# A hybrid trunk layer on one core: the first block normalised in two halves of 256 tokens, and the steps' chain moved beside the first pair of weight tiles

## The chip, the core and the metric

The kernel runs on one core of a Trainium2 chip. The metric is the device time of one execution in microseconds (us). Engines are named PE (TensorE), DVE (VectorE), ACT (ScalarE), POOL (GpSimd) and SP (SyncE, which issues all the DMAs here). PEld is PE's loading of weights, which overlaps its products.

## The reference

One layer on 2048 tokens of width 1024, all in float32:

```
h    = rmsnorm(x, norm_mix_w)
u_b, u_c, u_h, z, xbc, dt_raw = split(h @ w_in)
y_a  = u_b * conv3(u_c * u_h)                        # short gated convolution
xbc  = silu(conv4(xbc) + b);  dt = softplus(dt_raw + dt_bias)
y_b  = rmsnorm((ssd_scan(xs, dt, -exp(a_log), B, C) + d_skip * xs) * silu(z))
x    = x + concat(y_a, y_b) @ w_out
x    = x + relu(rmsnorm(x, norm_mlp_w) @ w_up)**2 @ w_down
out  = rmsnorm(x, final_norm_w)
```

where `rmsnorm(x, w) = x / sqrt(mean(x*x) + 1e-5) * w`.

## The kernel before

Channels lie on the 128 partitions, tokens along a tile. Tokens are worked in blocks of 512 (TB), two blocks to a half (TH = 1024). A float32 operand is split into a high part, rounded to a reduced form that PE takes in one pass (float32r), and the rest as a low part; one product is then three matmuls: high by high, low by high, high by low (`mm3`). Weight tiles are loaded whole (`load_w`), ACT casts the high part (`split_w`, line 103) and DVE subtracts to get the low part (line 104). Activations are split the same way (`split`, lines 204 and 205).

Most of the input projection works on *pairs* of weight tiles with seven products instead of eight per 2x2 block (`chain`), in the order of the list `PAIRS`: 'ch' pairs make the short convolution's input, 'x' pairs the four-tap convolution's (`conv`), 'b' and 'z' pairs the gates. For each pair the next pair's weights are combined and split (`weights`, `combine`). Beside the first pairs `prepare` normalises the second half's blocks, one step after each of the seven products of a pair (`late` in `first_half`); in the last pair of the list the blocks of the next half are fetched and split (`refresh`).

Before the first pair stands `start`: it loads x block 0, three weight tiles (z columns 24 to 26), squares block 0 on ACT, adds the squares on DVE, and sums over partitions on PE with `ones` as the moving column (`Rstd.reduce`). `Rstd.root` takes the root on ACT and the reciprocal on DVE, splits it into two float32r parts and spreads each over a diagonal; `Rstd.spread` turns the diagonals into a row that is alike in all partitions, with two matmuls, and copies it to SBUF. The block is multiplied by that row and split, eight tiles one after another. Then PE multiplies three weight tiles at once for block 0 (`group`), a fourth with its own accumulator, and the same for block 1; `begin_block(1)` normalises block 1 beside it and `begin_sums` builds the sums of blocks that the seven products want. `dt_part` is the chain of the steps (dt): 16 narrow products on PE, transposes, a softplus of some 25 small DVE operations, decays, and stores; block 0's chain runs inside `start`, block 1's mostly beside the first pair.

At the end `norm_out` uses the same `root` and `spread` for the final norm of the last block and of its two last halves of 256 tokens.

The order on each engine is made by a scheduler from the order in which the program writes the instructions, and from what it takes each to last. The pool `utmp` has four buffers, `e` five, `wraw` three; PSUM's eight banks are named mm (three), mw, yo, yd (one each) and tp (two).

Of the kernel before, what the change touches and what calls it, by code (L numbers as in the profile page):

```python
# [16 lines left out]
P = 128  # L17
T = 2048
# [21 lines left out]
def trunk(ctx: ExitStack, tc: tile.TileContext, x, w_in, w_dt, w_out, w_up, w_down, cvec, hrow, out):  # L40
# [31 lines left out]
    nc.sync.dma_start(cv[:, 0:NCV], cvec)  # L72
# [12 lines left out]
    nc.scalar.copy(cv[:, NCV + 1 : NCV + 2], eps)  # L85
# [21 lines left out]
    def take(it, n=None):  # L107

        return list(itertools.islice((w for w in it if w is not None), n))

# [10 lines left out]
    class Rstd:  # L121
# [18 lines left out]
        def root(self):  # L140
            n = self.n
            r = self.pool.tile([P, n], F32, tag="rs", name="rs", bufs=2)
            nc.scalar.activation(r, self.sums, AF.Sqrt, bias=eps, scale=self.scale)
# [4 lines left out]
            self.diag = []  # L148
            for i in range(2):
                diag = self.tmp("diag")[:, 0 : self.w].bitcast(F32R)  # L150
                nc.vector.tensor_tensor(
                    out=diag.rearrange("p (c t) -> p c t", c=n),
                    in0=ident.unsqueeze(1).to_broadcast([P, n, P]),
                    in1=r2[:, i, :].bitcast(F32).unsqueeze(2).to_broadcast([P, n, P]),
                    op=ALU.mult,
                )
                self.diag.append(diag)
# [16 lines left out]
        def spread(self, rb=None):  # L174
            prb = self.ps = psum("tp", "prb", 2)[:, 0 : self.w]
            for i in range(2):
                nc.tensor.matmul(prb, ones_r, self.diag[i], start=(i == 0), stop=(i == 1))
# [12 lines left out]
    class Seven:  # L190
# [10 lines left out]
        def split(self, pair, i, t):  # L201

            hi, lo = (x[:, i] for x in pair)
            nc.scalar.copy(hi, t)  # L204
            nc.vector.tensor_tensor(out=lo, in0=t, in1=hi.bitcast(F32), op=ALU.subtract)
# [92 lines left out]
        def fill(self, n, k, t):  # L298
# [5 lines left out]
            self.split(p[i], j, t)  # L304
# [99 lines left out]
    class Proj(Seven):  # L404
# [4 lines left out]
        PAIRS = "ch0 ch1 b0 x0 x8 ch2 ch3 b2 x2 ch4 ch5 b4 x4 x10 ch6 ch7 b6 x6 z4 z6".split()  # L409
# [41 lines left out]
        def begin_block(self, bb):  # L451
# [4 lines left out]
            for m, t in enumerate(xt):  # L456
                if bb == 0:
                    sq = self.wide("sq")
                    nc.scalar.activation(sq, t, AF.Square)
                    sq = [sq[:, 0], sq[:, 1]]  # L460
                else:
                    sq = [acc if m + i == 0 else self.tmp("sq") for i in range(2)]
                    for i in range(2):
                        nc.scalar.activation(sq[i], t[:, i], AF.Square)
                if m == 0:
                    nc.vector.tensor_tensor(out=acc, in0=sq[0], in1=sq[1], op=ALU.add)
                else:
                    for i in range(2):
                        nc.vector.tensor_tensor(out=acc, in0=acc, in1=sq[i], op=ALU.add)
# [6 lines left out]
            for k in range(KD):  # L476
# [4 lines left out]
                self.fill(("b11", "b21", "b12", "b22")[2 * bb + k // 4], k % 4, t)  # L481
# [29 lines left out]
        def group(self, bb, ws, tiles, work, tag="mm"):  # L511

            pm = [psum(tag, "pm", accs[tag]) for _ in tiles]
            for k in range(KD):
                for p, i in zip(pm, tiles):
                    mm3(p, ws[i][0][:, k, :], ws[i][1][:, k, :], *self.block(bb, k), k, KD)
                next(work, None)
            for p, i in zip(pm, tiles):
                o = self.tmp("z")
                nc.scalar.activation(o, p, AF.Silu)  # L520
                nc.sync.dma_start(sz_d[0][:, i, bb * TB : (bb + 1) * TB], o)

        def start(self):

            self.xt = [[self.raw("x0") for _ in range(KD // 2)], []]
            for k, t in zip(range(0, KD, 2), self.xt[0]):
                nc.sync.dma_start(t, x[0, :, k : k + 2])
            ahead = self.plain(w_in, (24, 25, 26))
            next(ahead)
            work = self.begin_block(0)  # L530
            for m in range(KD // 2):
                next(work)
# [5 lines left out]
            ws = []  # L538
            for _ in range(3):
                ws += take(ahead, 1)  # L540
                next(work)
            self.dt_weights()
            for _ in work:
                pass
            work = self.begin_block(1)
            last = self.plain(w_in, (27,))
            next(last)
            for bb in range(NBB):
                dts = self.dt_part(bb)
                self.group(bb, ws, (0, 1, 2), work)  # L550
                if bb == 0:
                    ws += take(last)
                    self.group(bb, ws, (3,), work, "mw")
                    self.bias()
                    for _ in dts:
# [1079 lines left out]
```

## Time and profile before

| what | value |
|---|---|
| median of 3 runs | 2649.1 us (2647.37 to 2652.85) |
| the profiled execution | 2645.76 us, span 2643.8 us from its first to its last instruction |
| PE busy | 2596.8 us, 98% |
| DVE, ACT, POOL busy | 74%, 54%, 2% |
| DMA | 511.78 MB, 58.5% of 16 engines' span |

Busy times are sums of instructions; those of PE are modelled at their ends and overlap their successors, so how fast PE works is read from the distance of two starts. An idle stretch of PE is the place where time can be lost or won; the rows below say where such stretches are and what the neighbouring operations last.

### The profile page before, as it was taken

How to read it: one execution, taken by the hardware profiler on the slowest of the kernel's cores; microseconds unless marked ns; L12 is line 12 of the kernel's file. 1: busy time of each engine (PE TensorE's matmuls, PEld its weight loads, DVE VectorE, ACT ScalarE, POOL GpSimd, SP SyncE). 2: the span in 40 equal slices, each digit the busy share in tenths (PEclk: the TensorE clock that was granted, in tenths of full speed). 3: DMA queues.
4: the chain of work that ended last, by engine and by line, in shares of the span. 5: the costliest groups of instructions: out<-in, count | busy, mean ns of one | idle time of the engine just before them, and what ended most of it. 6: DMA issues, size and time to landing. Idle time of an engine off the chain costs nothing.

```text
span 2643.8 us, 33439 instructions
## 1 busy us (share of the span) xinstructions
PE 2596.8 (98%) x12026; PEld 2122.1 (80%) x12026; DVE 1944.1 (74%) x2650; ACT 1423.3 (54%) x2150; POOL 54.2 (2%) x98
## 2 busy tenths in 40 slices
PE   7999999999999999999999999999999999999998
PEld 5778888778878888888888888788887888888887
DVE  7997676767777777768767765755558877888885
ACT  6644345777567666666326555655555444444443
POOL 0000010000000000000000000000000000000001
PEclk9999999999999999999999999999999999999999
DMA  3585344655555478967666674744448554665762
GB/s 146 189 300 193 138 149 169 212 157 167 160 170 181 153 243 272 290 208 229 211 209 213 234 271 139 260 158 143 163 148 287 162 150 149 212 207 181 238 206 70
DMA packets 284806, 511.78 MB, mean 194 GB/s; under 512 B 25312, under 2 KB 141024, under 8 KB 284640
## 3 DMA queue, kind: packets, MB, share of 16 engines
q1 hardware_dynamic: 284640, 509.65, 58.5%
q8 instruction: 94, 1.54, 0.2%
q14 instruction: 72, 0.59, 0.1%
HBM read 344.41 MB, written 165.15 MB: 193 GB/s over the span
## 4 chain that ended last, share of the span: by engine, by line
PE 65%; issue 25%; DVE 3%; DMA 3%; ACT 3%; SPq 0%; POOL 0%; POOLq 0%; DVEq 0%; ACTq 0%
PE px L269 9%; PE px L271 9%; PE px L270 9%; PE pm L112 5%; PE pm L113 5%; PE pm L114 5%; PE py L269 4%; PE py L271 4%; PE py L270 4%; PE pw L269 2%; PE pw L271 2%; PE pw L270 2%; PE yd L1266 1%; PE st L1263 1%; PE yo L1261 1%
## 5 line engine op out<-in xcount | busy, mean ns | idle before, releaser
L269 PE MATMUL px<-uh,whi 128*128 128x512 f32 x1672 | 656.7, 393 | 11.7 <-ACT pw L277 4.8
L271 PE MATMUL px<-uh,wlo 128*128 128x512 f32 x1672 | 651.8, 390 | 1.8 <-DVE wlo L104 1.8
L270 PE MATMUL px<-ul,whi 128*128 128x512 f32 x1672 | 651.5, 390 | 0.0
L104 DVE TENSOR_TENSOR wlo<-wraw,whi 128x1024 fp32r<-128x1024 f32 x230 | 233.6, 1016 | 205.5 <-ACT whi L103 199.3
L269 PEld LDWEIGHTS px<-uh,whi 128*128 128x128 f32 x1672 | 314.0, 188 | 86.5 <-ACT pw L277 7.8
L271 PEld LDWEIGHTS px<-uh,wlo 128*128 128x128 f32 x1672 | 314.1, 188 | 68.9 <-DVE wlo L104 2.7
L270 PEld LDWEIGHTS px<-ul,whi 128*128 128x128 f32 x1672 | 314.2, 188 | 63.5
L103 ACT CAST whi<-wraw 128x1024 fp32r<-128x1024 f32 x230 | 203.4, 885 | 276.3 <-PE px L270 188.0
L103 ACT CAST whi<-s 128x1024 fp32r<-128x1024 f32 x210 | 219.6, 1046 | 234.3 <-PE pw L270 77.7
L269 PE MATMUL py<-uh,whi 128*128 128x512 f32 x836 | 327.3, 392 | 1.8 <-DVE acc L986 1.4
L270 PE MATMUL py<-ul,whi 128*128 128x512 f32 x836 | 325.4, 389 | 0.0
L271 PE MATMUL py<-uh,wlo 128*128 128x512 f32 x836 | 325.3, 389 | 0.0
L104 DVE TENSOR_TENSOR wlo<-s,whi 128x1024 fp32r<-128x1024 f32 x210 | 255.4, 1216 | 84.9 <-ACT whi L103 81.7
L112 PE MATMUL pm<-uh,whi 128*128 128x512 f32 (+1 forms) x648 | 252.6, 391 | 2.1 <-ACT uh L204 2.1
L113 PE MATMUL pm<-ul,whi 128*128 128x512 f32 (+1 forms) x648 | 248.9, 384 | 0.0
L114 PE MATMUL pm<-uh,wlo 128*128 128x512 f32 (+1 forms) x648 | 248.4, 383 | 0.0
L269 PEld LDWEIGHTS py<-uh,whi 128*128 128x128 f32 x836 | 156.9, 188 | 36.1 <-DVE acc L986 1.8
L271 PEld LDWEIGHTS py<-uh,wlo 128*128 128x128 f32 x836 | 156.8, 188 | 32.9
L270 PEld LDWEIGHTS py<-ul,whi 128*128 128x128 f32 x836 | 157.0, 188 | 32.2 <-issue 0.2
L269 PE MATMUL pw<-uh,whi 128*128 128x512 f32 x418 | 163.6, 391 | 0.7 <-ACT pw L277 0.7
L270 PE MATMUL pw<-ul,whi 128*128 128x512 f32 x418 | 163.0, 390 | 0.0
L319 ACT CAST uh<-rh 128x1024 fp32r<-128x1024 f32 (+1 forms) x128 | 120.4, 944 | 78.9 <-PE py L271 62.4
(226 smaller groups left out, 3710.6 us busy)
## 6 DMA issues: line engine op xcount, KB each, us to landing
hid_d<-e SPq DMA_DIRECT2D x96, 512.0 KB, 3.7
rh<-hid_d SPq DMA_DIRECT2D x96, 512.0 KB, 4.4
wraw<-w_in SPq DMA_DIRECT2D x68, 512.0 KB, 4.1
wraw<-w_up SPq DMA_DIRECT2D x64, 512.0 KB, 4.4
wraw<-w_down SPq DMA_DIRECT2D x104, 256.0 KB, 3.7
dec<-rd_d SPq DMA_DIRECT2D x32, 512.0 KB, 5.7
wraw<-w_out SPq DMA_DIRECT2D x32, 512.0 KB, 5.4
x_d<-xt SPq DMA_DIRECT2D x64, 256.0 KB, 3.8
```

The source lines that it names most:

```text
L103: nc.scalar.copy(hi, raw)
L104: eng.tensor_tensor(out=lo, in0=raw, in1=hi.bitcast(F32), op=ALU.subtract)
L112: nc.tensor.matmul(out, whi, hi, start=(k == 0), stop=False)
L113: nc.tensor.matmul(out, whi, lo, start=False, stop=False)
L114: nc.tensor.matmul(out, wlo, hi, start=False, stop=(k == nk - 1))
L269: nc.tensor.matmul(p, hi, h[0], start=bool(first and k == 0), stop=False, **kw)
L270: nc.tensor.matmul(p, hi, h[1], start=False, stop=False, **kw)
L271: nc.tensor.matmul(p, lo, h[0], start=False, stop=(k == len(g) - 1), **kw)
L319: nc.scalar.copy(p[i][0], t)
L1261: nc.tensor.matmul(yo[:, j * L : (j + 1) * L], state[:, j * P : (j + 1) * P], cT, start=True, stop=True)
L1263: nc.tensor.matmul(st, t["btok"], t["xde"], start=True, stop=True)
L1266: nc.tensor.matmul(yd[(i % 2) * 64 : (i % 2) * 64 + 64, (i // 2) * L : (i // 2 + 1) * L], byhead(t["xdt"])[:, i, :], t["dec"][:, i, :], st ...
```

## The change

- Block 0 is loaded and normalised in two halves of 256 tokens (`begin_half`). The constants' load is moved behind the first half of x, the three weights behind that, then the second half.
- Squares are added in pairs on DVE, and four times two matmuls sum them over partitions in PSUM, instead of a running sum on DVE.
- `root` makes one float32 diagonal instead of two float32r ones, and `spread` one float32 matmul; in the halves the row is read from PSUM with no copy. This `root` and `spread` are those of block 1 and of the final norm too.
- `group` takes a slice of tokens: the first three weight tiles meet block 0 in two halves, the first of them with all products of the low weights last (`late`), the second in the accumulators mw, yo, yd. The evictions are put off (`gate`).
- 40, 12 and 16 matmuls of `ones_r` by itself, whose result nobody reads, are put on PE at the start, before the spread and before the first products.
- The queues' first orders are written out: `after(...)` puts an instruction behind a given one of its engine.
- The first activation, which loads a function table, is a root instead of a copy.
- Both blocks' step chains give only their products and the copy of the result inside `start`; their later steps run one after each product of the first pair and of the second, and the next norm's steps follow after them.
- The pair z4 moves from the last but one place of `PAIRS` to the first.

```diff
-    nc.sync.dma_start(cv[:, 0:NCV], cvec)
-    nc.scalar.copy(cv[:, NCV + 1 : NCV + 2], eps)
+    nc.scalar.activation(cv[:, NCV + 1 : NCV + 2], eps, AF.Sqrt)
...
+    @contextmanager
+    def after(marks):
+        with ExitStack() as stack:
+            for m in marks if isinstance(marks, tuple) else [marks] if marks is not None else []:
+                stack.enter_context(tc.issue_after(m.ins))
+            yield
...
         def root(self):
-            r2 = self.pool.tile([P, 2, n], F32R, tag="rs2", name="rs2", bufs=2)
-            nc.vector.tensor_copy(r2[:, 0, :], r)
-            nc.vector.tensor_tensor(out=r2[:, 1, :], in0=r, in1=r2[:, 0, :].bitcast(F32), op=ALU.subtract)
-            for i in range(2): ...
+            self.diag = self.tmp("diag")[:, 0 : self.w]
+            self.spreads = nc.vector.tensor_tensor(
+                out=self.diag.rearrange("p (c t) -> p c t", c=n),
+                in0=ident.unsqueeze(1).to_broadcast([P, n, P]),
+                in1=r.unsqueeze(2).to_broadcast([P, n, P]),
+                op=ALU.mult,
+            )
...
         def spread(self, rb=None, copy=True):
-            for i in range(2):
-                nc.tensor.matmul(prb, ones_r, self.diag[i], start=(i == 0), stop=(i == 1))
+            nc.tensor.matmul(prb, ones, self.diag, start=True, stop=True)
+            if not copy:
+                return prb
...
-        PAIRS = "ch0 ch1 b0 x0 x8 ch2 ch3 b2 x2 ch4 ch5 b4 x4 x10 ch6 ch7 b6 x6 z4 z6".split()
+        PAIRS = "z4 ch0 ch1 b0 x0 x8 ch2 ch3 b2 x2 ch4 ch5 b4 x4 x10 ch6 ch7 b6 x6 z6".split()
...
+        def begin_half(self, ts, behind=None):
+            st = self.st = Rstd(self.up, self.tmp, D, HB)
+            pst = psum("tp", "pst", 2)
+            for m, t in enumerate(self.xt[0]):
+                sq = self.tmp("sq").rearrange("p (a t) -> p a t", a=2)
+                with after(behind and behind[4 + m]):
+                    nc.scalar.activation(sq, t[:, :, ts], AF.Square)
+                    nc.vector.tensor_tensor(out=sq[:, 0], in0=sq[:, 0], in1=sq[:, 1], op=ALU.add)
+                for c in range(st.n):
+                    nc.tensor.matmul(pst[:, c : c + 1], sq[:, 0, c * P : (c + 1) * P], ones[:, 0:1], ...)
+                yield
+            st.sums = pst[:, 0 : st.n]
+            st.root()
+            yield
+            r = st.spread(copy=False)
+            self.filled = []
+            for k in range(KD):
+                t = self.xt[0][k // 2][:, k % 2, ts]
+                nc.vector.scalar_tensor_tensor(
+                    out=t, in0=t, scalar=col(C_NMIX, k), in1=r, op0=ALU.mult, op1=ALU.mult
+                )
+                self.filled.append(self.fill(("b11", "b21")[k // 4], k % 4, t, ts))
+                yield
...
         def start(self):
+            load(ends[0])
+            nc.sync.dma_start(cv[:, 0:NCV], cvec)
+            raws = [load_w(w_in[f]) for f in (24, 25, 26)]
+            load(ends[1])
...
+            idle(WARM[0])                                  # WARM = (40, 12, 16)
+            work = self.begin_half(ends[0])
+            for m in range(KD // 2):
+                next(work)
+            hi_part(0, ends_w[0])
+            next(work)
+            idle(WARM[1])
+            with after(self.st.spreads):
+                lo_part(0, ends_w[0])
+            with after(self.st.rooted):
+                hi_part(0, ends_w[1])
+                hi_part(1)
+            next(work)
+            idle(WARM[2])
+            next(work)
+            next(work)
+            with after(self.filled[1][0]):
+                hi_part(2)
+            for _ in work:
+                pass
+            first = self.filled
+            with after(first[-1][1]):
+                lo_part(0, ends_w[1])
+                lo_part(1)
+                lo_part(2)
+            self.dt_weights()
+            raws.append(load_w(w_in[27]))
+            work = self.begin_half(ends[1], first)
+            gates = [self.group(0, ws, (0, 1, 2), work, ts=ends[0], late=True)]
+            for _ in work:
+                pass
+            second = self.filled
+            with after(second[5][0]):
+                hi_part(3)
+            with after(second[-1][1]):
+                lo_part(3)
+            work = self.begin_block(1, second)
+            with after(second[-1][0]):
+                gates.pop()()
+            gates.append(self.group(0, ws, (0, 1, 2), work, ("mw", "yo", "yd"), ends[1]))
+            gates.append(self.group(0, ws, (3,), work))
+            for g in gates:
+                g()
+            dts = [self.dt_part(bb) for bb in range(NBB)]
+            next(dts[0])
+            for _ in work:
+                pass
+            work = self.begin_sums()
+            gate = self.group(1, ws, (0, 1, 2), work)
+            gate()
+            ahead = self.weights(0, self.PAIRS[0])
+            next(ahead)
+            next(dts[1])
+            with after(second[-1]):
+                got = take(ahead, 3)
+                self.bias()
+            gate = self.group(1, ws, (3,), work, ("mw",))
+            gate()
+            with after(second[-1]):
+                got += take(ahead)
+            for _ in work:
+                pass
+            self.dts = itertools.chain(*dts)
...
                 def after(name):
-                    next(late, None)
+                    if next(self.dts, "end") == "end":
+                        next(late, None)
```

In `begin_block(1)` the squares of block 1 and their additions stand behind every second tile of the second half (`after(behind[2 * m + 1])`).

## Rows read from the trace of the kernel before

**Rows 1.** The page's busy times: us (share of the span) xinstructions.

```profile
PE 2596.8 (98%) x12026; PEld 2122.1 (80%) x12026; DVE 1944.1 (74%) x2650; ACT 1423.3 (54%) x2150; POOL 54.2 (2%) x98
```

**Rows 2.** Stretches: length, busy PE, PEld, DVE, ACT, POOL, clock, DMA share, GB/s.

```profile
19.59:25.30 5.71, 5.71 (x13) 4.41 (x14) 5.71 (x11) 3.81 (x7) 0.00 (x0) 1.00 0.45 160
25.30:76.39 51.09, 51.09 (x236) 39.34 (x234) 44.31 (x90) 32.39 (x54) 2.33 (x1) 1.00 0.18 61
...
76.39:446.75 370.36, 366.62 (x1609) 300.15 (x1608) 283.28 (x361) 168.10 (x215) 26.17 (x38) 1.00 0.53 189
140.00:205.00 65.00, 62.08 (x268) 49.51 (x267) 58.57 (x76) 30.53 (x39) 6.83 (x9) 1.00 0.91 329
...
446.00:486.00 40.00, 38.08 (x174) 31.10 (x174) 30.12 (x37) 29.43 (x45) 0.31 (x2) 1.00 0.84 277
```

**Rows 3.** Timeline of the opening: start, us, engine, line, op, what, idle before.

```profile
7.04 1.06 ACT L459 ACTIVATE sq<-x 128x1024 f32<-128x1024 f32 x1 [0.22 <-DMA x<-x]
...
9.60 1.06 ACT L459 ACTIVATE sq<-x 128x1024 f32<-128x1024 f32 x1 [0.23 <-DMA x<-x]
...
12.64 1.86 PE L131 MATMUL pst<-ones_r,facc 128*128 128x1 f32 x8 [12.64 <-DVE facc L469]
...
14.55 0.26 ACT L143 ACTIVATE rs<-pst,cv 128x4 f32<-128x4 f32 x1 [1.33 <-PE pst L131]
...
19.59 1.65 PE L112 MATMUL pm<-uh,whi 128*128 128x512 f32 x3 [2.11 <-ACT uh L204]
```

**Rows 4.** Timeline of block 0's group: the first and last of 31 products.

```profile
26.52 0.40 PE L112 MATMUL pm<-uh,whi 128*128 128x512 f32 x1
...
33.34 0.39 PE L112 MATMUL pm<-uh,whi 128*128 128x512 f32 x1
```

**Rows 5.** Timeline near the end: operations of 256 columns; products first and thirteenth.

```profile
2608.85 0.28 PE L112 MATMUL pm<-uh,whi 128*128 128x256 f32 x1
...
2610.29 0.28 PE L112 MATMUL pm<-uh,whi 128*128 128x256 f32 x1
...
2622.72 0.75 DVE L1066 TENSOR_TENSOR acc<-pm,acc 128x256 f32<-128x256 f32 x2
...
2626.45 0.75 DVE L151 TENSOR_TENSOR diag<-ident,rs 128x256 fp32r<-128x256 f32 x2
...
2627.76 0.37 ACT L180 COPY rstd<-prb 128x256 f32<-128x256 f32 x1 [1.05 <-PE prb L177]
...
2628.17 0.87 DVE L1084 SCALAR_TENSOR_TENSOR acc<-acc,cv,prb 128x256 f32<-128x256 f32 x2 [0.15 <-ACT rstd L180]
```

**Rows 6.** Float32 products: timeline of block 1's sums; the scan's 512 columns, ns.

```profile
38.78 0.95 PE L131 MATMUL pst<-ones_r,facc 128*128 128x1 f32 x8
...
39.59 0.48 PE L112 MATMUL pm<-uh,whi 128*128 128x512 f32 x1
...
L1263 PE MATMUL st<-stmp,btok x64: 590/594/668, 486.7 to 1262.3; 128*128 128x512 f32 x64
```

**Rows 7.** Timeline: the first product of the first pair.

```profile
76.39 0.50 PE L269 MATMUL px<-uh,whi 128*128 128x512 f32 x1
```

**Rows 8.** Timeline of ACT: four of the copies that follow each pair's first product.

```profile
159.16 0.57 ACT L277 COPY pw<-px 128x512 f32<-128x512 f32 x1 [0.80 <-PE px L271]
...
181.93 0.59 ACT L277 COPY pw<-px 128x512 f32<-128x512 f32 x1
...
449.48 0.57 ACT L277 COPY pw<-px 128x512 f32<-128x512 f32 x1 [1.88 <-PE px L271]
...
470.85 0.59 ACT L277 COPY pw<-px 128x512 f32<-128x512 f32 x1
```

**Rows 9.** Groups of lines beside the first pairs: busy us, mean ns, idle before.

```profile
L663 DVE SCALAR_TENSOR_TENSOR cacc<-buf,cv,cacc 128x1024 f32<-128x1024 f32 x12 | 15.3, 1278 | 0.0
...
L104 DVE TENSOR_TENSOR wlo<-wraw,whi 128x1024 fp32r<-128x1024 f32 x3 | 3.7, 1222 | 0.2 <-ACT whi L103 0.2
...
L356 DVE TENSOR_TENSOR facc<-facc,lx 128x512 f32<-128x512 f32 x12 | 8.2, 685 | 0.0
```

More of the change, by code (lines that the diff above doesn't have):

```diff
@@ L1 @@
 import itertools
-from contextlib import ExitStack
+from contextlib import ExitStack, contextmanager
 import numpy as np
@@ L456, in begin_block @@
             for m, t in enumerate(xt):
[L457 to L462, printed above, removed]
+                sq = [acc if m + i == 0 else self.tmp("sq") for i in range(2)]
+                with after(behind[2 * m + 1]):
                     for i in range(2):
                         nc.scalar.activation(sq[i], t[:, i], AF.Square)
[L465 to L469, printed above, removed]
+                    if m == 0:
+                        nc.vector.tensor_tensor(out=acc, in0=sq[0], in1=sq[1], op=ALU.add)
+                    else:
+                        for i in range(2):
+                            nc.vector.tensor_tensor(out=acc, in0=acc, in1=sq[i], op=ALU.add)
                 yield
@@ L509, in begin_sums, with group, product @@
                     yield
-        def group(self, bb, ws, tiles, work, tag="mm"):
-            pm = [psum(tag, "pm", accs[tag]) for _ in tiles]
+        def group(self, bb, ws, tiles, work, tags=("mm",), ts=slice(0, TB), late=False):
+            w = ts.stop - ts.start
+            pm = [psum(tag, "pm", accs.get(tag, 1))[:, 0:w] for tag, _ in zip(itertools.cycle(tags), tiles)]
+            block = [[t[:, ts] for t in self.block(bb, k)] for k in range(KD)]
+            def product(p, i, k, part):
+                weights, moving = ((0, 0), (0, 1), (1, 0))[part]
+                nc.tensor.matmul(
+                    p,
+                    ws[i][weights][:, k, :],
+                    block[k][moving],
+                    start=(k == 0 and part == 0),
+                    stop=(k == KD - 1 and part == 2),
+                )
@@ L514, in group @@
             for k in range(KD):
                 for p, i in zip(pm, tiles):
-                    mm3(p, ws[i][0][:, k, :], ws[i][1][:, k, :], *self.block(bb, k), k, KD)
+                    for part in range(2 if late else 3):
+                        product(p, i, k, part)
                 next(work, None)
[L518 to L521, printed above, removed]
+            if late:
+                for p, i in zip(pm, tiles):
+                    for k in range(KD):
+                        product(p, i, k, 2)
@@ L528, in start, with load @@
[L528 to L532, printed above, removed]
+            def load(ts):
+                for k, t in zip(range(0, KD, 2), self.xt[0]):
+                    nc.sync.dma_start(t[:, :, ts], x[0, :, k : k + 2, ts])
+            load(ends[0])
+            nc.sync.dma_start(cv[:, 0:NCV], cvec)
+            raws = [load_w(w_in[f]) for f in (24, 25, 26)]
+            load(ends[1])
@@ L536, in start, with hi_part @@
                 self.xt[1].append(t)
-            next(work)
[L538 to L542, printed above, removed]
+            pairs = [wtile() for _ in range(4)]
+            ws = [[t.rearrange("p (k c) -> p k c", k=KD) for t in pair] for pair in pairs]
+            both = slice(0, 1024)
+            ends_w = [slice(0, 512), slice(512, 1024)]
+            def hi_part(n, cs=both):
+                nc.scalar.copy(pairs[n][0][:, cs], raws[n][:, cs])
@@ new lines, in lo_part, with idle @@
+            def lo_part(n, cs=both):
+                hi, lo = pairs[n]
+                nc.vector.tensor_tensor(
+                    out=lo[:, cs], in0=raws[n][:, cs], in1=hi[:, cs].bitcast(F32), op=ALU.subtract
+                )
+            warm = psum("tp", "warm", 2)
+            def idle(n):
+                for _ in range(n):
+                    nc.tensor.matmul(warm[:, 0:P], ones_r, ones_r, start=True, stop=True)
+            idle(WARM[0])
+            work = self.begin_half(ends[0])
@@ L604, in dt_part @@
                 )
[L605 removed]
+            dts = t[0:32, TB : 2 * TB]
             nc.scalar.copy(dts, pd[0:32, :])
```

79 lines of the change are left out of this document (30 added, 49 removed).

## Prediction

> **What bounds the kernel now.** I read the page's busy times first: PE is busy 98% of the span [rows 1], so only stretches where PE stands, runs slowly, or gets more to do can move the time. The table by stretches [rows 2] shows which. PE's first product of a weight tile starts at 19.59 [rows 3]; up to there PE waits for one chain. Then 13 products of 512 columns take 5.71 us, 0.44 each, while later ones start 0.227 apart (30 in 6.82 us [rows 4]): the lower and the upper clock level by their pace, though the clock column reads 1.00. From 25.30 to the first pair at 76.39 [rows 7] PE's busy time equals the stretch: no wait. The 19 pairs from there to 446.75 take 370.4; 19 x 84 products x 0.227 are 362.8 [rows 2, 4], so 7.6 are lost there, by estimate 1.9 of them to small products of the steps' chain and the next norm, some 5.7 to waits. The largest wait is in one pair: 159.16 to 181.93 is 22.8 where 19.1 would do; the last pair of the first half (449.48 to 470.85) loses 2.3 [rows 8]. Between 140 and 205 DVE is busy 58.6 of 65 us and DMA 0.91.
>
> The opening chain [rows 3]: half of x (1 MB) is there at 7.04, the last quarter at 9.60, when its square starts; adds on DVE hold the sums to 12.64, PE needs 1.86 for them, the root starts at 14.55; roots, two diagonals, two spreading products, a copy, a multiplication and a cast follow until 19.59.
>
> **The change, part by part.** The sum is made against the profiled execution (2645.76 us, span 2643.8); the median of the runs shown, 2649.1, lies 3.3 above it, and I add the same 3.3 to the forecast.
>
> *Earlier first product: -7.6.* Only 256 tokens, 1 MB, are needed first, and the constants' load stands behind them: 6.8 instead of 7.04 for that amount. Then: square of 512 elements 0.6 (half of the 1.06 row, and a start), one 256-column add 0.4 (two in 0.75 [rows 5]), the last four sum products 0.6 (eight in 0.81 at the upper level, from 38.78 to 39.59 [rows 6], and their way out), root 0.26, reciprocal 0.2 (estimate), one diagonal 0.4 (two in 0.75), the spread 0.5, multiplication from PSUM 0.45, cast 0.37 [rows 5], ten hand-overs of 0.04 as between 14.50 and 14.55 [rows 3]: 11.0. The 12 and 16 idle products stand in PE's queue between these steps; at 0.12 each they take 1.4 and 1.9, mostly beside root, diagonal, multiplication and cast; left over is 0 to 1.4. The first 40 take 4.8 to 8.8 from about 1.2, so they end between 6 and 10, around the first sums: 0 to 2.5. The first cast of a weight half also stands ahead of the root on ACT. I take 1.0 for all of it: 12.0, range 11.0 to 14.9.
>
> The fp32 spread is not in the trace of before at this size. A 128x512 fp32 product shows as two instructions of 0.594 where the reduced form has 0.39 [rows 6]; for 256 columns I take 0.5 (bounds: 0.24, as two reduced ones at 0.12, and 1.19).
>
> *The clock: -2.8.* 13 products in 5.71 would be 2.95 at 0.227. The idle products keep PE at work from the start, so I expect the upper level from 12.0 on. If not, nothing is gained here (bound 0; the dearer case is a rival).
>
> *More work for PE: +3.5.* 256-column products start 0.12 apart (12 in 1.44 [rows 5]), so 144 of them cost 0.9 more than 72 whole ones. The second half's sums are 16 instructions of 0.1, 1.6, and its spread 0.5, both in the stream. Block 1's spread goes from two reduced products (0.45) to fp32 (about 1.0): 0.5.
>
> *DVE behind two halves: +1.5.* From 12.0 PE alone would need 17.3 + 2.1, to 31.4. DVE begins to multiply at about 10.7. A tile costs it 0.43 (two in 0.87) and 0.38; eight cost 6.5, four adds of the second half's squares 1.5, the last tile's lag 0.5: 19.2. The weight low parts follow (1.22 each [rows 9], two and a half: 3.0), reciprocal and diagonal 0.6: 22.8. The second half: 6.5 and five adds of block 1 at 0.68, 9.9: 32.7, and 0.7 of products: 33.4, two late. With overlapped starts (0.40 and 0.34 instead) 32.4, one late. I take 1.5; range 0 to 3.5, the upper end if the fourth weight's low part stands behind two more adds.
>
> *The steps' chain.* Its transposes and sums (about 1.3 of PE) and some 25 small operations on DVE go from before the first pair to beside it and the next: the same work, PE gains nothing. On DVE it takes the place of the next norm's steps, which start ten steps later. Gates' Silu and the chain's Exp alternate in that pair; each swap costs ACT a table load, and ACT, busy 54% of the span [rows 1], has room. Taken as 0; without that cover it is one late eviction of about a load per swap. The casts and stores that are moved on SP's queue end long before PE asks for them; were the fourth weight late, tile 3 would wait, and 3.7 us of step products stand behind it as no cover.
>
> *Order of the pairs: -2.0 and +1.2.* z4 has no convolution, so DVE starts ch0 without the backlog of the opening; x0 and x8, beside the next norm's tiles, stay overloaded, and DMA stays full. Of the 5.7 of waits I take 2.0 away (range -4 to +1.5). At the other end x6 now stands directly before the last pair: three DVE passes of 1.28 [rows 9], 3.8 us, and two ACT passes move into the pair that refills the blocks. DVE idles 9.9 of 40 us there [rows 2]; I charge 1.2 (0 to 3.8).
>
> *The tail: +0.5.* The final norm uses the same spread: two fp32 spreads in PE's last stretch, 0.55 for 512 columns and 0.26 for 256 more than the reduced pairs: +0.8; two small DVE operations and a diagonal fewer in the closing chain: -0.3 (estimate).
>
> Sum: -7.6 - 2.8 + 3.5 + 1.5 - 2.0 + 1.2 + 0.5 = -5.7. So 2640.1 profiled, 2643.4 timed, 0.2% faster.
>
> **Rivals.**
> *B, given back later.* Where DVE and DMA are the bound (140 to 205), an earlier PE only waits longer. For: DVE 58.6 of 65. Against: z4 brings 19 us of PE with about 8.4 us of DVE (weights' low parts 3.5 x 1.22, six half-width additions at 0.68). If 4 come back there: -1.7, 2647.4.
>
> *C, the halves of x arrive hardly earlier.* They are cut into rows a quarter as long. If each half load takes as long as a whole one, the last lands at 9.2 (0.4 of issue earlier than 9.60): +2.4, -3.3, 2645.8. Against: the quarters land 1.28 apart, as fast as all queues together carry, so bytes count, not loads. The Trainium skill, "DMA: Bandwidth & Descriptors", section "Measured (HBM→SBUF, 128 partitions, SWDGE, issued from GpSimd)", speaks against small loads: batch to 1 MiB, 2.0 us fixed and then bytes by 436 GB/s, for another issuing path. By it four 256 KB loads one after another would take 10.4 us, and as an estimate from that page the sum would be about -1. The trace, with loads in flight together, does not show this.
>
> *E, the last pair.* If x6's passes are paid in full, +3.8 instead of +1.2: -3.1, 2646.0.
>
> *D, the other side: PE stays at the lower level through the halves.* In half 1 PE waits for DVE at every tile, as before 25.30. A 256-column product then costs about 0.22 instead of 0.12: 144 x 0.10 = 14.4, of which 1.5 hide behind DVE: +12.9, so +7.2, 2656.3. It turns the sign when 72 of the 144 run so, and makes it 0.2% slower at 125. Against: 28 idle products just before, and DVE and PE nearly in step. [...]
>
> **How the numbers follow.** A measurement of this kernel tells about 0.2%, 5.3 us, from no change. Forecast A 0.64: its terms spread over 2638 to 2647, so 0.52 lies beyond 5.3 faster, 0.12 within. B 0.12, C 0.08, E 0.06: all within. D 0.10: slower. Faster 0.52, same 0.38, slower 0.10. The range 2637.5 to 2650.5 holds A but for its lowest end, and B, C and E; D is left out.
>
> **What would show it.** In the changed profile: the first weight product at 11 to 13 with starts 0.12 apart from there (else D, or C if the last quarter's square starts after 8.5); the second half's last product at 32 to 34; the first pair at 69 to 71 instead of 76.4; no pair up to the third over 20 us; the pair after x6 at 22 to 24. The forecast is wrong if the first pair starts before 67 or after 73, or if the x pairs lose over 7 us.

## The result, and the profile after

The changed kernel takes 2654.5 us (median of 11 runs, 2651.1 to 2659.6) beside 2647.1 for the kernel before (11 runs, the three shown above among them): 1.0033 times as long, 95% interval 1.0025 to 1.0042. It is slower by 0.33%, where 0.2% faster was forecast (2643.4 us, range 2637.5 to 2650.5). Its profiled execution took 2658.46 us (span 2656.6).

The page's busy times, which answer to [rows 1]:

```profile
PE 2616.3 (98%) x12192; PEld 2144.2 (81%) x12192; DVE 1941.2 (73%) x2655; ACT 1426.1 (54%) x2166; POOL 66.8 (3%) x98
```

PE is busy 19.5 us longer, and 15.5 of that are the idle products. The timeline of PE's opening (start, us, engine, line, op, what), and one row of DVE's and two of ACT's, beside [rows 3]:

```profile
1.12 8.80 PE L615 MATMUL warm<-ones_r 128*128 128x128 f32 x40 [1.12 <-DVE cv L85]
9.72 3.51 PE L467 MATMUL pst<-ones_r,sq 128*128 128x1 f32 x16
13.09 2.80 PE L615 MATMUL warm<-ones_r 128*128 128x128 f32 x12
15.69 1.16 PE L179 MATMUL prb<-diag,ones_r 128*128 128x256 f32 x2
16.29 3.87 PE L615 MATMUL warm<-ones_r 128*128 128x128 f32 x16
19.96 0.52 PE L553 MATMUL pm<-uh,whi 128*128 128x256 f32 x1
...
22.18 0.28 PE L553 MATMUL pm<-uh,whi 128*128 128x256 f32 x1
```

```profile
8.40 0.43 DVE L465 TENSOR_TENSOR sq<-sq 128x256 f32<-128x256 f32 x1 [0.31 <-ACT sq L464]
...
13.27 0.26 ACT L152 ACTIVATE rs<-pst,cv 128x2 f32<-128x2 f32 x1 [3.47 <-PE pst L467]
...
17.41 0.80 ACT L209 CAST uh<-x 128x256 fp32r<-128x256 f32 x2 [2.42 <-DVE x L483]
```

The idle products are 0.22 apart (40 in 8.80 us), not 0.12. PE takes its instructions in order: the sums of the squares start only when the 40 are through, though the first of them have had their operand since about 4.9 and the last since 8.8 (DVE's last addition); the root waits for the sums, the spread starts behind the next 12, and the first weight product, whose operand the cast at 17.41 has made by about 17.8, starts behind the last 16. It starts at 19.96; before it was 19.59.

The stretches that answer to [rows 2] (same columns):

```profile
19.96:22.18 2.22, 2.22 (x12) 2.22 (x12) 2.22 (x7) 1.25 (x4) 0.00 (x0) 1.00 0.00 0
22.18:80.92 58.74, 55.77 (x317) 45.62 (x315) 48.37 (x87) 35.77 (x65) 10.86 (x1) 1.00 0.23 77
80.92:451.70 370.78, 369.35 (x1632) 303.81 (x1631) 283.69 (x379) 172.23 (x221) 28.19 (x40) 1.00 0.53 189
451.70:477.31 25.61, 22.02 (x96) 17.56 (x94) 23.16 (x22) 20.65 (x25) 1.84 (x2) 1.00 0.81 264
```

Up to 22.18 the products of 256 columns are 0.21 apart, the lower clock level (1.2 GHz) by their pace, though the clock column reads 1.00 in every stretch here; then 0.12, the upper (2.4 GHz). In the second stretch, where PE had no wait before, it now stands 3.0 us. The first pair starts at 80.92, 4.5 later than [rows 7]. The timeline of all engines where PE stands:

```profile
40.43 1.28 ACT L444 ACT_TABLE_LOAD   x1
...
43.77 2.72 ACT L498 ACTIVATE sq<-x 128x512 f32<-128x512 f32 x5 [1.31 <-DMA sz_d<-z]
...
44.44 3.88 DVE L503 TENSOR_TENSOR facc<-facc,sq 128x512 f32<-128x512 f32 x5 [1.25 <-ACT sq L498]
...
47.12 0.39 PE L553 MATMUL pm<-uh,wlo 128*128 128x512 f32 x1
...
48.47 1.02 PE L140 MATMUL pst<-ones_r,facc 128*128 128x1 f32 x8 [0.96 <-DVE facc L503]
...
50.79 1.12 PE L179 MATMUL prb<-diag,ones_r 128*128 128x512 f32 x2 [1.29 <-DVE diag L155]
...
51.35 0.79 PE L711 MATMUL pd<-uh,wdt 128*32 128x512 f32 x1
```

Tile 3 is the fourth weight tile on block 0, whose last product starts at 47.12. Block 1's squares wait on ACT behind the load of a table for the bias's Exp (40.43), and then for small buffers that the put-off evictions hold until their stores have landed (1.31 before 43.77). So block 1's additions end at 48.3, after the last product of tile 3. Its sums and its spread stand in PE's queue ahead of the 16 step products (pd), and PE waits 0.96 for the one and 1.29 for the other: 2.25 of the 3.0.

From the first pair to the last pair of the first half 370.8 pass instead of 373.1: 2.3 come back in this profile. Then ACT's copies after the first product of a pair, beside [rows 8]:

```profile
451.70 0.57 ACT L283 COPY pw<-px 128x512 f32<-128x512 f32 x1 [0.51 <-PE px L277]
...
477.31 0.58 ACT L283 COPY pw<-px 128x512 f32<-128x512 f32 x1
```

The last pair takes 25.6 instead of 21.4. At 477 the changed kernel is 6.5 behind.

### The profile page after: what moved, and what is told of

It is laid out like the page before. It is cut to its first block, busy times and chain, and to the rows that moved or that the text cites. A ratio compares the mean times of both kernels' runs of the same rounds, so it can differ in the third digit from the quotient of the medians.

```text
span 2656.6 us, 33807 instructions
## 1 busy us (share of the span) xinstructions
PE 2616.3 (98%) x12192; PEld 2144.2 (81%) x12192; DVE 1941.2 (73%) x2655; ACT 1426.1 (54%) x2166; POOL 66.8 (3%) x98
## 4 chain that ended last, share of the span: by engine, by line
PE 65%; issue 25%; DMA 4%; DVE 3%; ACT 2%; SPq 0%; POOL 0%; POOLq 0%; DVEq 0%; ACTq 0%
PE px L275 9%; PE px L277 9%; PE px L276 9%; PE py L275 4%; PE py L276 4%; PE py L277 4%; PE pm L121 4%; PE pm L123 4%; PE pm L122 4%; PE pw L275 2%; PE pw L276 2%; PE pw L277 2%; PE pm L553 1%; PE yd L1376 1%; PE st L1373 1%
## 5 line engine op out<-in xcount | busy, mean ns | idle before, releaser
L121 PE MATMUL pm<-uh,whi 128*128 128x512 f32 (+1 forms) x584 | 227.0, 389 | 0.0
L122 PE MATMUL pm<-ul,whi 128*128 128x512 f32 (+1 forms) x584 | 223.0, 382 | 0.0
L123 PE MATMUL pm<-uh,wlo 128*128 128x512 f32 (+1 forms) x584 | 222.8, 381 | 0.0
```

The costliest lines, as they stand in the source:

```text
L121: nc.tensor.matmul(out, whi, hi, start=(k == 0), stop=False)
L122: nc.tensor.matmul(out, whi, lo, start=False, stop=False)
L123: nc.tensor.matmul(out, wlo, hi, start=False, stop=(k == nk - 1))
```

## The experiments

One table for all. The runs of before that a ratio rests on were made beside it; their medians lay between 2641.3 and 2647.1. "Last pair" is the distance of the two copies just shown, "rest" the span from the second of them to the end; times are in us and those of the profiled execution.

| run | ratio to before (95%) | first weight product | first pair | last pair | rest |
|---|---|---|---|---|---|
| before | 1 | 19.59 | 76.39 | 21.4 | 2173.0 |
| changed | 1.0033 (1.0025 to 1.0042) | 19.96 | 80.92 | 25.6 | 2179.3 |
| e1 | 1.0012 (1.0003 to 1.0021) | 12.80 | 80.00 | 24.5 | 2171.6 |
| e2 | 1.0037 (1.0023 to 1.0051) | 19.95 | 83.98 | 22.2 | 2174.7 |
| e3 | 0.9995 (0.9985 to 1.0005) | 12.38 | 77.36 | 21.4 | 2170.2 |
| e4 | 1.0015 (1.0005 to 1.0025) | 20.00 | 76.77 | 24.6 | 2173.7 |
| e5 | 0.9989 (0.9980 to 0.9998) | 12.54 | 76.31 | 21.2 | 2172.8 |
| e6 | 0.9992 (0.9984 to 1.0001) | 12.49 | 78.71 | 21.2 | 2165.8 |
| e7 | 0.9992 (0.9984 to 1.0001) | 12.62 | 75.68 | 22.0 | 2170.2 |
| e8 | 0.9991 (0.9983 to 1.0000) | 11.98 | 75.04 | 21.9 | 2169.8 |
| e9 | 0.9963 (0.9950 to 0.9975) | 12.60 | 71.07 | 22.2 | 2170.4 |
| e10 | 1.0030 (1.0021 to 1.0040) | 19.95 | 83.55 | 24.6 | 2172.5 |
| e11 | 1.0017 (1.0005 to 1.0028) | 19.96 | 77.02 | 22.3 | 2173.9 |
| e12 | 0.9977 (0.9967 to 0.9988) | 13.05 | 72.09 | 25.4 | 2166.9 |

**Parts alone, e1 to e4.** e1 takes the idle products out of the changed kernel, e2 gives it the old list of pairs, e3 does both, and e4 gives the kernel before the new list.

```diff
-WARM = (40, 12, 16)                                     # e1, e3
+WARM = (0, 0, 0)
-PAIRS = "z4 ch0 ch1 ... b6 x6 z6"                       # e2, e3 (e4: the other way)
+PAIRS = "ch0 ch1 ... b6 x6 z4 z6"
```

> The changed kernel without its 68 idle products (nothing else of the order differs beyond the opening). Theory W (the idle products run 0.22 apart at the lower clock level and stand in PE's queue ahead of the sums, the spread and the first products): sums done at about 9.7, spread at 11, first weight product at 13 to 14 instead of 19.96; the clock then rises later after the first product than the 2.2 us of the changed kernel (before took 5.7), so some 1 to 2 are given back; first pair near 76 instead of 80.9, time 4 to 5.5 us under the changed kernel, that is ratio to before 1.001 to 1.002. Rival R1 (the idle products are what raises the clock): with none, PE stays at 0.21 a product through the first half-block, loses up to 6 again, and the first pair stays at 80 to 81; ratio 1.003. Rival R2 (DVE is the bound of the opening): first product earlier, but PE waits as much more behind DVE, first pair at 79 to 81.

> The changed kernel with the list of pairs of before (z4 last but one). Theory O (x6 directly before the last pair costs 4, z4 first brings 2): the last pair of the first half takes 21.4 to 22 instead of 25.6, the pairs to there give back the 2.3 they regained; time 2 us under the changed kernel, ratio 1.0025. Rival (the refill of the blocks is dear in any order in the changed kernel): the last pair stays at 25, time 2 us above the changed kernel, ratio 1.004. Rival (the regain is not from z4 at all): the last pair at 21.4, the middle keeps its gain, 4 under the changed kernel, ratio 1.0015.

> No idle products and the list of pairs of before. If W and O both hold and add: 6 to 7.5 us under the changed kernel, the time of before within 2 us, ratio 0.9998 to 1.0005; what is left of the opening's loss (first pair at about 76 with a first product 6 earlier) is then in block 1's chain, where PE stands from 47.4 on. If later stages lose by themselves (the growth from +6.5 at 477 to +13 at the end in the profiled pair is real), the ratio stays at 1.002 and the milestones from 978 on lag before's by 4 or more beyond the lag at 477.

> The kernel before with one part of the change alone: z4 moved to the front of the list. Theory O: the pairs up to the last one lose 2 less, the last pair takes 25 instead of 21.4, so 2 us slower than before, ratio 1.0007. As predicted blind (-2.0 and +1.2): 0.8 faster, ratio 0.9997. If the new order costs only together with the moved steps' chain: the last pair stays at 21.4 to 22 and the time is 2 under before, ratio 0.999.

W (the idle products hold up what stands behind them): without them the first weight product starts at 12.4 to 12.8, 7.2 to 7.6 earlier, and the ratio falls by 0.002 from the changed kernel to e1 and by 0.004 from e2 to e3. But e1's first pair starts at 80.00, where W expected about 76 and its rivals 79 to 81: only 0.9 of the 7.2 is left against the first profile of the changed kernel, and 3.6 against its second (e10). In e3 the first pair is still 1.0 behind before. Part of what was won is lost again on the way, which the next runs take up.

O (the order of the pairs): in e4, one part of the change by itself, the last pair goes from 21.4 to 24.6 and the kernel is 0.15% slower, some 4 us; the pairs before it regain 0.7 (76.77 to 449.14 instead of 76.39 to 449.48). From e1 to e3 the ratio falls by a like 0.0017 (the intervals overlap a little). e2 alone is no faster than the changed kernel, where O expected 1.0025; that value lies inside the wide interval of its six runs, so this run neither bears O's price out nor refutes it. Its last pair is 22.2 again; its opening is as long as e10's, and one pair near 225 to 250 took 26.3, in e3 23.5. In the profiles the two lists stay apart: the last pair takes 24.5 to 25.6 in all five with z4 first, and 21.2 to 22.3 in all nine with the old list. Where the last pair's time goes, the changed kernel's DVE, ACT and PE show (timelines), beside the same place on DVE before:

```profile
450.23 4.87 DVE L772 SCALAR_TENSOR_TENSOR cacc<-buf,cv,cacc 128x1024 f32<-128x1024 f32 x4
455.01 1.22 DVE L326 TENSOR_TENSOR ul<-rb,uh 128x1024 fp32r<-128x1024 f32 x1
456.14 1.28 DVE L772 SCALAR_TENSOR_TENSOR cacc<-buf,cv,cacc 128x1024 f32<-128x1024 f32 x1
...
477.44 1.23 DVE L326 TENSOR_TENSOR ul<-rb,uh 128x1024 fp32r<-128x1024 f32 x1 [1.67 <-ACT uh L325]
```

```profile
451.19 4.63 DVE L320 TENSOR_TENSOR ul<-rb,uh 128x1024 fp32r<-128x1024 f32 x4 [2.95 <-ACT uh L319]
```

```profile
476.36 1.04 ACT L325 CAST uh<-rb 128x1024 fp32r<-128x1024 f32 x1 [1.63 <-DMA rb<-hm_d]
...
477.94 0.50 PE L275 MATMUL px<-uh,whi 128*128 128x512 f32 x1 [3.62 <-ACT pw L283]
```

Five of the six passes of x6's convolution (L772), 6.2 us, stand ahead of or between the first subtractions that refill the blocks (L326). Before, four subtractions ran from 1.7 behind the pair's copy on (451.19 behind 449.48); now the first starts 3.3 behind it (455.01 behind 451.70) and the next three after the fifth pass. The refill stays late. Near its end one of its casts waits 1.63 for a load; the copy that PE needs stands behind that cast in ACT's queue (477.31), and PE waits 3.6 before it can go on in the next half's first pair. That wait is 3.3 in e4 and 3.6 in e12, and before has none at this place. Two activations of x6 on ACT moved into this pair too; the runs don't tell their share from DVE's.

**Where the opening loses, e5 to e8.** The base is e3. e5 gives the put-off evictions a buffer of their own and moves the bias with its Exp behind block 1's root; e6 takes the steps' raw weights out of the small buffers; e7 does both; e8 adds to e7 eight idle products of 512 columns.

```diff
-                    o = self.tmp("z")[:, 0:w]                                # e5, e7, e8
+                    o = self.tmp("z")[:, 0:w] if z is None else z[:, i * w : (i + 1) * w]
-                gates.pop()()
+                gates.pop()(self.e("z"))
-                self.bias()             # behind the second half's last cast
+            with after(self.st1.rooted):
+                self.bias()             # at the end of start
-            raw = self.tmp("rdt")[:, 0 : KD * 16]                            # e6, e7, e8
+            raw = (self.tmp if self.h else self.e)("rdt")[:, 0 : KD * 16]
-WARM = (0, 0, 0)                                                             # e8
+WARM = (8, 0, 0)                        # moving operand: ones_r four times, 512 columns
```

> The kernel without idle products and with the old list of pairs (the base here: ratio 0.9995), plus: the three put-off evictions of the first half-block go to a buffer of their own instead of three of the four small ones, and the load of the bias with its Exp stands after block 1's root. Theory K (block 1's squares wait for the stores of those evictions, 1.58 us, and for a table load and an Exp, 1.5 us, so its sums, root and spread end behind the last product of tile 3 and PE stands from 44.9 to 47.7): the sums start in the middle of tile 3, PE has no wait of over 0.5 us between tile 3 and the first pair, the first pair starts 2 to 2.5 earlier than the base's 77.36; time 2 to 2.5 us under the base, ratio 0.9985 to 0.999. Rival (block 1 is bound by its five additions on DVE, not by the waits): the sums start where they were, no change.

> The same base, plus: the raw weights of the steps go to another buffer, so that the fourth square of the second half-block need not wait for a small one. Theory H (the square at 23.69 waited 5.03 us for a buffer that the second half's own sums give back, and by it PE waits 1.0 for the diagonal and 1.0 for the first cast between the halves, after which 17 products run 0.21 apart instead of 0.12): the fourth square starts near 19, the second half's sums and root end before 24, PE passes from half 1 to half 2 without a wait of over 0.7, and the clock stays at its upper level; first pair 3 to 5 us earlier than 77.36, time 3 to 5 under the base, ratio 0.9977 to 0.9984. Rival (DVE's own work, not the buffer, sets the second half): the waits stay at 2 us in sum, gain under 1.

> Both repairs on the same base. K and H together: first pair at 70 to 72, 5 to 7 us under the base's 77.36, time 5 to 7 under the base, ratio 0.997 to 0.9977, faster than before and than the changed kernel. Rival (B of the prediction: where DVE and DMA are the bound, beside the first pairs, what came earlier is given back): first pair at 71, but the last pair of the first half starts less than 3 us earlier than the base's 449.7.

> Both repairs, and eight idle products of 512 columns ahead of the first sums (nobody reads them). If wide products without a wait raise the clock where the narrow ones did not: they run 0.43 apart from 1.1 to 4.6, the sums start at 5 as without them, and the first weight products start 0.12 apart from the first on; time 1 to 2 us under the kernel with both repairs alone. If what PE does before the first weight product doesn't matter to the clock: products 0.21 apart for 2 to 5 us again, as in every profile so far, and the time of the kernel with both repairs within 1 us. If they hold the sums up: first weight product later than 12.4.

K (block 1's chain comes too late) holds in the profile. e5's timeline of PE:

```profile
43.10 0.95 PE L140 MATMUL pst<-ones_r,facc 128*128 128x1 f32 x8
46.27 1.02 PE L179 MATMUL prb<-diag,ones_r 128*128 128x512 f32 x2
46.72 0.79 PE L713 MATMUL pd<-uh,wdt 128*32 128x512 f32 x1
```

The sums lie inside tile 3 and the spread follows its last product without a wait. In e3 both stand behind that product:

```profile
44.94 0.95 PE L140 MATMUL pst<-ones_r,facc 128*128 128x1 f32 x8
47.18 1.12 PE L179 MATMUL prb<-diag,ones_r 128*128 128x512 f32 x2 [1.29 <-DVE diag L155]
```

From the end of tile 3 to the first pair e5 needs 30.04 (46.27 to 76.31) and e3 32.42 (44.94 to 77.36). But 0.8 of these 2.4 is the sums, which are now paid inside tile 3. The first pair starts 1.05 earlier than in e3, not 2 to 2.5, and the ratio moved by only 0.0006, inside the intervals. So the mechanism is shown and its price was taken too high; which of e5's two moves matters more isn't separated.

H (the second half waits for a buffer) fell: e6 and e7 still wait between the halves. e6's first pair starts at 78.71, 1.4 later than e3's, and e7's at 75.68, where 70 to 72 was expected. DVE and PE in e7 (timelines):

```profile
20.87 1.09 DVE L465 TENSOR_TENSOR sq<-sq 128x256 f32<-128x256 f32 x3
25.54 0.17 DVE L153 RECIPROCAL rs<-rs 128x2 f32<-128x2 f32 x1 [3.58 <-ACT rs L152]
```

```profile
24.71 0.50 PE L467 MATMUL pst<-ones_r,sq 128*128 128x1 f32 x4
...
26.29 0.70 PE L179 MATMUL prb<-diag,ones_r 128*128 128x256 f32 x2 [0.85 <-DVE diag L155]
28.00 1.01 PE L554 MATMUL pm<-uh,whi 128*128 128x256 f32 x3 [1.01 <-ACT uh L209]
```

The additions are over at 21.96, with the buffer free. Then DVE does nothing for 3.6 us, because the last sums stand in PE's queue behind products of the first half until 24.71. After the two waits 22 products run 0.21 apart. So the rival was as wrong as H: neither a buffer nor DVE's work set the second half, PE's order did, as e9 shows below.

e8 is no faster than e7. The wide idle products didn't hold the sums up, and the sums behind them ran faster, but not the weight products:

```profile
1.12 3.70 PE L617 MATMUL warm<-ones_r 128*128 128x512 f32 x8 [1.12 <-DVE cv L85]
4.98 1.32 PE L467 MATMUL pst<-ones_r,sq 128*128 128x1 f32 x8 [0.17 <-DVE sq L465]
6.89 0.60 PE L467 MATMUL pst<-ones_r,sq 128*128 128x1 f32 x4 [0.58 <-DVE sq L465]
7.79 0.85 PE L467 MATMUL pst<-ones_r,sq 128*128 128x1 f32 x4 [0.29 <-DVE sq L465]
...
11.98 0.80 PE L554 MATMUL pm<-uh,whi 128*128 128x256 f32 x2 [1.01 <-ACT uh L209]
...
13.65 0.41 PE L554 MATMUL pm<-uh,whi 128*128 128x256 f32 x1
```

Behind them eight sums take 1.32, where they take 1.86 without; after four waits the first weight products are 0.21 apart again, 22 of them.

**Everything in step, e9 to e12.** e9 is e7 with the second half's sums, root and spread ahead in program order. e10 is the changed kernel once more, e11 is e9 with the idle products, e12 is e9 with the new list.

```diff
-            with after(first[-1][1]):
-                lo_part(0, ends_w[1]); lo_part(1); lo_part(2)
+            with after(first[-1][1]):
+                lo_part(0, ends_w[1])
...
             work = self.begin_half(ends[1], first)
+            for m in range(KD // 2):
+                next(work)
+            with after(first[-1][1]):
+                lo_part(1)
+            next(work)
+            with after(self.st.spreads):
+                lo_part(2)
+            next(work)
```

> The kernel with both repairs, and the second half's sums, root and spread put ahead in program order: its four additions and its reciprocal and diagonal stand on DVE before the low parts of the second and third weight, so that PE's sums and spread stand 10 products earlier in its queue. Theory H2 (between the halves PE waits 0.85 for the diagonal and 1.01 for the first cast because its own queue held the sums to 24.7, though the additions were done at 21.96 and DVE then stood idle to 25.5): no wait of over 0.5 us between the halves, the second half's first product at 25 to 26 instead of 28.0, and as PE doesn't stand, no products at the lower level after it (22 in the kernel with both repairs, 2 us); first pair at 71 to 73.5 instead of 75.7; ratio to before 0.9975 to 0.9985. Rival (DVE's low parts come too late for the first half's last products once they are moved back): PE waits as long for the third weight's low part, first pair at 75 or later.

> The changed kernel once more, unaltered, beside the others. If the difference is made in the opening and the last pair of the first half, its lead over before at 477 us (+6.5 in the profiled pair) accounts for the whole of the difference of medians: ratio 1.0025 to 1.0035 again, and the stretch from the second half's first pair to the end lasts 2170 to 2176 as in all other profiles (2179 in the first profile of it). If later stages lose by the change: that stretch is again 2178 or longer.

> The kernel with the halves in step, and the changed kernel's 40, 12 and 16 idle products put back. Theory W: the first weight product goes from about 12.4 back to 20, the first pair 5 to 7 later, ratio 0.002 to 0.0027 above that of the kernel without them. Rival (they pay for themselves by the clock, so that what they cost without a repair was only the waits behind them): first pair less than 2 us later.

> The kernel with the halves in step, with the changed kernel's list (z4 first, x6 directly before the last pair). Theory O: the last pair of the first half takes 24.5 to 25.6 instead of 21.2 to 22, and no more than 1.5 comes back in the pairs before it; 2 to 3.5 us slower than the kernel with the halves in step, ratio 0.0008 to 0.0013 above it. Rival (as forecast blind, -2.0 and +1.2): 0.8 faster.

e9 beats both kernels: 0.37% faster than before (six runs), where 0.15 to 0.25% was expected. Its timeline of PE, from the second half's spread to the first pair:

```profile
10.37 1.22 PE L179 MATMUL prb<-diag,ones_r 128*128 128x256 f32 x2 [1.12 <-DVE diag L155]
12.60 0.80 PE L554 MATMUL pm<-uh,whi 128*128 128x256 f32 x2 [1.01 <-ACT uh L209]
...
24.11 2.00 PE L554 MATMUL pm<-uh,wlo 128*128 128x256 f32 x11
25.95 0.52 PE L554 MATMUL pm<-uh,whi 128*128 128x256 f32 x3
...
34.59 0.40 PE L554 MATMUL pm<-uh,whi 128*128 128x512 f32 x1
...
71.07 0.39 PE L275 MATMUL px<-uh,whi 128*128 128x512 f32 x1
```

The second half follows the first with no wait, at 0.12, and ends at 34.6; the first pair starts at 71.07, 4.6 earlier than in e7 and 5.3 earlier than before.

e11 puts the idle products back. The first weight product is at 19.96 and the first pair at 77.02, 5.95 later; the ratio rises by 0.0054, twice what was expected. The profiles differ by 12.5 in all: 5.95 to the first pair, 3.1 in the pairs up to and with the last, and 3.5 in the rest. Only the 5.95 is traced to the idle products. The other two lie inside the scatter of their stretches: the rest column shows its own, and from the first pair to the last the kernels with the old list took 370.4 to 374.3. e12 puts the new list back: the last pair takes 25.4 instead of 22.2, the pairs before it regain 0.9, the ratio rises by 0.0014 (the intervals overlap a little).

e10 settles what the first profile seemed to show of later stages. Its rest is 2172.5, as before's 2173.0. The 2179.3 of the first profile of the changed kernel was scatter: the other 13 profiles lie between 2165.8 and 2174.7. e10 is 7.2 behind before at the first pair, 4.5 at the last pair's start, 7.8 at 478.60 and 7.3 at the end, so the loss is made before 480. Its first pair is 2.6 later than in the first profile, and the rows of PE say why:

```profile
50.76 2.08 PE L179 MATMUL prb<-diag,ones_r 128*128 128x512 f32 x2 [1.29 <-DVE diag L155]
51.85 1.42 PE L711 MATMUL pd<-uh,wdt 128*32 128x512 f32 x1
53.06 0.63 PE L711 MATMUL pd<-ul,wdt 128*32 128x512 f32 x1
...
56.45 0.40 PE L711 MATMUL pd<-ul,wdt 128*32 128x512 f32 x1
```

After PE stood for block 1, the step products ran 0.43 apart here, the lower level, and 0.23 apart in the first profile. The two waits at that place cost 2.2 (0.88 and 1.29), and about 5 with what follows at the lower level: from the spread to the first product behind the step products 7.3 pass here, 4.65 in the first profile. The same happened in e1 and e2, not in e3.

## Why the prediction was wrong

The spread and the multiplication behind it in e3, without idle products (timelines of PE and of DVE), for the first point:

```profile
10.15 1.22 PE L179 MATMUL prb<-diag,ones_r 128*128 128x256 f32 x2 [1.11 <-DVE diag L155]
```

```profile
11.41 1.66 DVE L483 SCALAR_TENSOR_TENSOR x<-x,cv,prb 128x256 f32<-128x256 f32 x4 [0.71 <-PE prb L179]
```

- **Earlier first product, -7.6: the step that failed.** What failed is "I take 1.0 for all of it": the idle products held the first product back by 7.2 to 7.6, the whole gain. The working had priced the last 28 at 0.12, the upper level, and counted them as hidden. At 0.22 the 40 end at about 9.7, which the working allowed for ("between 6 and 10"), but then all 16 sums stood queued behind them and cost PE 3.5 at the lower level, where 0.6 was forecast for the last four alone. The range for the step, 11.0 to 14.9, left the measured 19.96 out. Without idle products the first product came at 12.4 to 13.05, where the steps of the chain add up to 11.0. The working had the order of the chain right, but its fp32 spread too short: from its start to the multiplication 1.26 pass in e3 (the rows above), where 0.5 was taken (bound 1.19). To the end the idle products cost 0.002 (changed kernel to e1), 0.004 (e2 to e3) and 0.0054 (e9 to e11, of which 5.95 us, 0.0023, are traced to them).
- **The clock, -2.8.** Forecast from the first weight product; in the changed kernel it came 2.2 us after (some 10 products at 0.09 too much instead of 13 at 0.21: 1.8 saved), in e2, with the same opening, only after 22 products. Without idle products it was 10 to 17, so they bought nothing here. Rival D, the lower level through all of the halves, didn't come either.
- **More work, +3.5, and DVE behind two halves, +1.5.** Together with the clock's -2.8 this made 2.2 between the first product and the first pair. The changed kernel lost 4.2 there (61.0 instead of 56.8), e9 only 1.7 (58.5). So the sum was about right for a kernel whose queues fit; the three terms weren't measured apart, and the clock's gave less than 2.8. The two differ by 2.5, and the changed kernel's waits for block 1's sums and spread come to 2.25. The working counted block 1's five additions as DVE's load, but not that its squares need buffers held by stores, nor that its sums and spread stand ahead of the step products in PE's queue. In e10 the lower level behind these waits made it 6.8 instead of 4.2.
- **The steps' chain, 0, and order of the pairs, -2.0.** The 2.3 that the pairs regained are no proof of the mechanism named. z4 at the front gives 0.7 (e4) and 0.9 (e12). The same stretch takes 369.5 to 373.0 in the five profiles with z4 first and 370.4 to 374.3 in those with the old list, so 2.3 in one profile is no more than the scatter. That the forecast's -2.0 came so near is luck.
- **x6 before the last pair, +1.2.** It measured 3.0 to 4.2, as in rival E (3.8, chance 0.06). The working counted three DVE passes and set them against DVE's idle time; there are six, and five of them don't take idle time but stand ahead of the refill, whose end holds the copy that PE waits for.
- **The tail, +0.5.** From the spread of 512 columns near the end to the last instruction 28.8 pass instead of 29.2: -0.3.
- **Rivals B and C.** x's half loads came in time (the last quarter's square starts at 7.00, C's sign was after 8.5), and what e9 wins before the first pair is not given back at 140 to 205: e9 is 5.3 ahead of before at the first pair and 8.0 at the last.

The sum to the first pair, 76.4 - 7.6 - 2.8 + 3.5 + 1.5 = 71.0, is what e9 does (71.07). That it agrees so closely is in part luck: e9's first product is 7.0 earlier, not 7.6, and the stretch behind it 1.7 longer, not 2.2. The forecast described a kernel whose idle products and queue orders don't get in its way. The changed kernel differs from e9 by 9.9 at the first pair, 5.95 for the idle products (by e11) and 3.9 for the queue orders; in the last pair it loses 2 to 3 more than the 1.2 forecast. Its second profile, e10, adds up: it is 13.0 over the forecast's -5.7, of which 12.5 lie before the first pair, -0.7 in the pairs to the last, 2.1 in the last pair and -1.0 behind it.

## What to carry to other kernels

Work put on an engine to keep it busy stands in that engine's in-order queue: price it at the slow pace it may run at, and ask what real instruction is next in the queue and when its operand is ready. When a chain is moved forward, follow where its small matmuls stand among the big ones, since a sum placed some ten products too late left DVE idle for 3.6 us and moved the first pair by 4.6 (e7 and e9). A pass moved beside a refill is priced by what queues behind it, not by the idle share of its engine.

## What the runs showed of the hardware

Sixty-eight products of 128 columns, back to back with only the sums and a spread between them, kept PE busy from 1.12 to 19.96 and left it at the lower level: the 16 sums between them were 0.21 apart (eight take 0.81 at the upper level [rows 6]), and after them 9 to 22 weight products of 256 columns were 0.21 apart instead of 0.12 (the changed kernel, e2, e10, e11). The narrow products were 0.22 apart themselves; no run shows what they take at the upper level. Without any, 10 to 17 weight products were at 0.21 (e1, e3, e5 to e7, e9, e12). Eight products of 512 columns did bring shorter sums behind them (1.32 instead of 1.86 for eight), and waits of 0.6, 0.3, 1.1 and 1.0 us later the products were 0.21 apart again. The Trainium skill, "TensorE: Matmul & The Clock Gate", section "Part 1: The HAM clock gate (the "warmup" mystery)", says that "activity releases the throttle". By that rule alone the narrow idle products would be expected to bring the upper level; this case's rows at 19.96 show the lower. What sets the level is not settled by these runs. In the other direction, two waits of about 1 us between the halves (0.85 and 1.01 in e7, the like in e1, e3, e5, e6 and e8) were followed by 12 to 24 products at the lower level: by estimate, at 0.09 a product, a second price of 1 to 2 us beside the waits' own.
